# First mixer's scan: the norm of a chunk in three steps behind later chunks' masked scores, and half of the gate's last products on GpSimd

## The chip, the core and the metric

The kernel runs on one core of a Trainium2 chip. The metric is the device time of one execution in microseconds; the time before is the median of three runs.

A core has five engines that each work through their own queue in order: TensorE (PE, its weight loads PEld), VectorE (DVE), ScalarE (ACT), GpSimd (POOL) and SyncE (SP), which here only issues DMA transfers. An instruction that waits holds everything behind it on its engine.

## What is computed

Two layers over 512 latent and 256 context tokens of width 1024: layer 0 mixes with a bidirectional mLSTM, layer 1 with retention, and a mixture of 16 experts follows each mixer. The change touches the end of the first mixer. Its scan sums a forward and a backward pass over chunks, norms every head's row, and gates:

```python
s = jnp.einsum('bhid,bhjd->bhij', qc, kc) * jnp.exp(dmat - m_row[..., None])
num = jnp.einsum('bhij,bhjv->bhiv', s, vc) + w_inter[..., None] * jnp.einsum('bhid,bhdv->bhiv', qc, C)
h = num / jnp.maximum(jnp.abs(den), jnp.exp(-m_row))[..., None]
...
y = y * lax.rsqrt(jnp.mean(y * y, axis=-1, keepdims=True) + EPS)
y = y.reshape(b_, t_, h_ * d_) * norm_g.astype(f32) * jax.nn.sigmoid(o.astype(f32))
return y.astype(o.dtype) @ w_out
```

## The kernel before

The stage lies at some 240 to 390 us of the span. Tokens are cut into six chunks of 128 (order 2, 3, 4, 5, 0, 1), heads into two halves of four (`blk` 0 and 1). In the text "chunk 0" to "chunk 5" count in that order, and a prime marks the second half: chunk 1' is the second chunk of `blk` 1.

`scan0` is a Python generator, one per half. The projections' loop (`Proj.run`) calls it after every step of eight, so its instructions are emitted among the projection's matmuls, the `acc` products (three of 128x512 per step and tile). The first half's scan runs beside the projection of the second half of V and the first gate half, then `states(1)`, then the second half's scan beside the gate's two halves. A scheduler of the language then sets the order on each engine; the lists below show its result.

For a chunk, the scan does this:

- `load` (SP): `qk`, `V`, the decay exponents `E` (two, one per direction) and the weights `qw`, each with two buffers; `load_states` brings the states `Cz`.
- `prep`: GpSimd masks `E` (`affine_select`, L711), ScalarE takes the exponential (eight L715, four per direction), VectorE makes `qw` (L717).
- `scores`: TensorE makes the scores `S0`, `S1` (L725, one buffer each), VectorE makes the masked scores `A0`, `A1` of both directions (four L731).
- `outputs`, once per direction: TensorE makes `num` (L739, L742; two buffers of `num0` and `num1`), VectorE the divisor (`dn`, `rd`: L748, L750, L751); the first direction's quotient `yo` is written by ScalarE (L755), the second's is added by VectorE (L757).
- `normed`: ScalarE squares `yo` (`ysq`, L762), VectorE sums (`yss`, L764, L765), GpSimd raises to the power -1/2 (`yrs`, L766), VectorE multiplies `yo` by it (L767), all emitted directly behind `outputs`.

`o_done` gates a finished tile of the gate's projection: ScalarE's sigmoid `oe` (L636, which frees the `acc` buffer; there are two), GpSimd's product with the norm's gain `ng` (L637), VectorE's product with `yo` (L638), and the store. Sigmoid and exponential need different tables on ScalarE, so a table load lies between them.

`states(1)` makes the second half's states: GpSimd `kw` (L612), TensorE `cu` (L618), VectorE `C` (L622, L624), ten in a row, then stored; `mixer_end` follows with the output projection, from the transposes `yt` on.

Of the kernel before, what the change touches and what calls it, by code (L numbers as in the profile page):

```python
# [2 lines left out]

# [11 lines left out]
OP = mybir.AluOpType  # L15
# [30 lines left out]
def backbone(ctx, tc, x, c, ctx_in, c_ctx, ada_w, ada_b, norm_mix_g, norm_ffn_g, final_norm_g,  # L46
# [3 lines left out]
    nc = tc.nc  # L50
# [5 lines left out]
    def st(name):  # L56
        return small.tile([128, 8], F32, name=name, tag="st", bufs=24)
# [22 lines left out]
    with tc.tile_pool(name="ps0", bufs=1, space=PS, reuse_waits="tile") as ps0, \  # L80
# [24 lines left out]
        for V, vc in ((V1, vc1), (V2, vc2), (VP[:, 0::2], vcp[:, :, 0]), (VP[:, 1::2], vcp[:, :, 1])):  # L105
            n = V.shape[0]
            p = ps0.tile([128, 64], F32, name="pv", bufs=2)
# [397 lines left out]
    order0 = (2, 3, 4, 5, 0, 1)  # L505

    def mlstm_mixer(R):
# [123 lines left out]
        Y, gated = {}, []  # L631

        def o_done(blk, ng):
            def f(tt, p):
                e = pc.tile([128, 512], F32, name="oe", bufs=2)
                nc.scalar.activation(e, p, AF.Sigmoid)  # L636
                nc.gpsimd.tensor_tensor(e, e, ng, op=OP.mult)  # L637
                nc.vector.tensor_tensor(e, e, Y[blk, tt].rearrange("p h v -> p (h v)"), op=OP.mult)  # L638
                nc.sync.dma_start(y_d[0][tt][:, blk * 512:(blk + 1) * 512], e)
                gated.append(tt)  # L640
            return f
# [13 lines left out]
        sb = ctx_w.enter_context(tc.tile_pool(name="scan0", bufs=2, side="right", reuse_waits="tile"))  # L655
        sp = ctx_w.enter_context(tc.tile_pool(name="scanps0", bufs=1, space=PS, side="right", reuse_waits="tile"))
        bg.add(scan0(0, sb, sp, pc, cols, flo, Y, gated), 2)
        P.run(1536, range(6), v_done(1), nxt=2048)
        bg.drain()
        bg.add(seq(states(1, sp, "num0"), scan0(1, sb, sp, pc, cols, flo, Y, gated)))  # L660
        for blk in range(2):
            ng = pc.tile([128, 512], F32, name="ng", bufs=1)
# [7 lines left out]
    def scan0(blk, sb, sp, pc, cols, flo, Y, gated):  # L670

        hs = slice(blk * 4, blk * 4 + 4)
        L = {}
# [6 lines left out]
        def load(cc):  # L680
            t = L[cc] = {}
            t["qk"] = sb.tile([128, 4, 128], F32, name="qk")
            nc.sync.dma_start(t["qk"], dram_ap(qk_d[blk], cc * 128, [[T, 128], [128 * T, 4], [1, 128]]))
            t["V"] = sb.tile([128, 4, 129], F32, name="V")
            nc.sync.dma_start(t["V"], V_d[blk][cc * 128:(cc + 1) * 128])
            t["E"] = sb.tile([128, 2, 4, 128], F32, name="E")
            for d in range(2):
                nc.sync.dma_start(t["E"][:, d], dram_ap(rows_d, (d * H + blk * 4) * T + cc * 128,
                                                        [[0, 128], [T, 4], [1, 128]]))
            ds = [d for d in range(2) if cc in prev0[d]]  # L690
            t["qw"] = sb.tile([128, 2, 2, 128], F32, name="qw")
            for d in ds:
                for h2 in range(2):
                    nc.sync.dma_start(t["qw"][64 * h2:64 * h2 + 64, d],
                                      dram_ap(rows_d, ((2 + d) * H + blk * 4 + h2) * T + cc * 128,
                                              [[0, 64], [2 * T, 2], [1, 128]]))

        def load_states(cc):
            C = L[cc]["C"] = CZ[order0.index(cc) % 2]
            for q in range(2):  # L700
                r = slice(64 * q, 64 * q + 64)
                for d in range(2):
                    if cc in prev0[d]:
                        nc.sync.dma_start(C[r, d, :, q, :], C_d[blk][cc][r, d].rearrange("p (a b) -> p a b", a=2))

        def prep(cc):
            t = L[cc]
            for d in range(2):
                E = t["E"][:, d]
                sg = 1 if d == 0 else -1  # L710
                nc.gpsimd.affine_select(out=E, in_=E, pattern=[[0, 4], [sg, 128]], compare_op=OP.is_ge, fill=BIG,  # L711
                                        base=0, channel_multiplier=-sg)
                for i in range(4):
                    h = blk * 4 + i
                    nc.scalar.activation(E[:, i, :], E[:, i, :], AF.Exp, bias=cols[:, cc, d, h:h + 1], scale=-1.0)  # L715
                if cc in prev0[d]:
                    nc.vector.scalar_tensor_tensor(t["qw"][:, d], t["qk"][:, 0:2], 0.125, t["qw"][:, d],  # L717
                                                   op0=OP.mult, op1=OP.mult)

        def scores(cc):  # L720
            t = L[cc]
            S = [sp.tile([128, 2, 128], F32, name=f"S{q}") for q in range(2)]
            for i in range(4):
                r = slice(64 * (i % 2), 64 * (i % 2) + 64)
                nc.tensor.matmul(S[i % 2][:, i // 2, :], t["qk"][r, 2 + i // 2, :], t["qk"][r, i // 2, :],  # L725
                                 start=True, stop=True)
            for d in range(2):
                A = t["A", d] = sb.tile([128, 2, 2, 128], F32, name=f"A{d}")
                Ev = t["E"][:, d].rearrange("p (g q) i -> p q g i", q=2)
                for q in range(2):  # L730
                    nc.vector.scalar_tensor_tensor(A[:, q], S[q], 0.125, Ev[:, q], op0=OP.mult, op1=OP.mult)  # L731

        def outputs(cc, d, y):
            t = L[cc]
# [22 lines left out]
                        nc.vector.scalar_tensor_tensor(y[:, i, :], num[j][:, q, 0:128], rd[:, q:q + 1], y[:, i, :],  # L757
                                                       op0=OP.mult, op1=OP.add)

        def normed(cc, y):  # L760
            j = sb.tile([128, 4, 128], F32, name="ysq", bufs=1)
            nc.scalar.activation(j, y, AF.Square)  # L762
            ss, rs = st("yss"), st("yrs")
            nc.vector.tensor_reduce(ss[:, 0:4], j, axis=mybir.AxisListType.X, op=OP.add)  # L764
            nc.vector.tensor_scalar(ss[:, 0:4], ss[:, 0:4], 1.0 / 128, EPS, op0=OP.mult, op1=OP.add)  # L765
            nc.gpsimd.tensor_tensor(rs[:, 0:4], ss[:, 0:4], neghalf[:, 0:4], op=OP.pow)  # L766
            nc.vector.tensor_tensor(y, y, rs[:, 0:4, None].to_broadcast([128, 4, 128]), op=OP.mult)  # L767
        load(order0[0])
        load_states(order0[0])
        yield 1  # L770
# [2 lines left out]
        prep(order0[0])  # L773
        yield 1
        scores(order0[0])
        yield 1
        for n, cc in enumerate(order0):
            if n + 2 < len(order0):
                load(order0[n + 2])
            if n + 1 < len(order0):  # L780
                prep(order0[n + 1])
                yield 3
                scores(order0[n + 1])
                yield 4
            while len(gated) < 6 * blk + n - 5:
                yield 1
            y = pc.tile([128, 4, 128], F32, name="yo", bufs=6)
            outputs(cc, 0, y)
            yield 1
            outputs(cc, 1, y)  # L790
            normed(cc, y)
            Y[blk, cc] = y
            if n + 2 < len(order0):
                load_states(order0[n + 2])
            yield 2

    def gates(P, pp, tt_, wgp, gb, cols, flo, wcb, colp):
        ig = tt_("ig")
# [1167 lines left out]
```

## Time and profile before

| | us |
|---|---|
| median of three runs | 1916.28 (1913.15 to 1919.35) |
| the profiled execution | 1921.03 |
| its span, first to last instruction | 1919.2 |
| TensorE busy over the span | 1814.5 (95%) |
| VectorE, ScalarE, GpSimd busy | 730.0, 429.1, 285.3 |
| TensorE busy from 246 to 390 us | 127.97 of 144.00 |

The page gives the busy shares; the waits say which engine waited for whom; a timeline row gives an instruction's start, its length, its engine and line, and in brackets how long the engine stood idle before it and what ended that. Time that an engine other than the bound one stands idle costs nothing by itself.

### The profile page before, as it was taken

The page shows a single profiled execution, that of the slowest core. Times are in us where ns is not written, and L with a number is a line of the kernel's source. Part 1 is how long each engine was busy: PE and PEld are TensorE (multiplying, and loading weights), DVE is VectorE, ACT ScalarE, POOL GpSimd, SP SyncE. Part 2 cuts the span into 40 slices and gives each one's busy share as a digit, 9 for nine tenths or more (in the row PEclk, how much of TensorE's full clock was granted, in tenths as well). Part 3 has the DMA queues.
Part 4 walks back from the last instruction along what each step waited for, and adds up shares of the span by engine and source line. Part 5 has one row for each costly group of instructions (what it writes and reads, how often), then busy time and mean ns, then how long its engine had stood idle before and what let it go on. Part 6 is the DMA issues. An engine that isn't in the chain of part 4 may idle for free. (4 is left out here: it accounts for less than half of the span.)

```text
span 1919.2 us, 27783 instructions
## 1 busy us (share of the span) xinstructions
PE 1814.5 (95%) x11093; PEld 1029.8 (54%) x11093; DVE 730.0 (38%) x1742; ACT 429.1 (22%) x839; POOL 285.3 (15%) x343
## 2 busy tenths in 40 slices
PE   6999988999899999999999999999979999999997
PEld 2765676788444434444444777788764333333332
DVE  3554557646311111111113678454571322222224
ACT  3623356342200000000003621332421010100001
POOL 1110124201121111111001224334200000000001
PEclk9999999999899999999999999999998999999999
DMA  8568777672899999999996588445738999999996
GB/s 273 209 210 273 261 190 206 197 270 84 303 368 391 383 388 398 377 401 379 407 412 234 194 291 274 130 153 188 285 154 306 421 421 420 421 421 421 421 420 247
DMA packets 168578, 585.42 MB, mean 305 GB/s; under 512 B 16674, under 2 KB 68578, under 8 KB 114690
## 3 DMA queue, kind: packets, MB, share of 16 engines
q1 hardware_dynamic: 160176, 570.72, 78.3%
q0 software_dynamic: 6912, 12.71, 3.1%
q8 instruction: 88, 1.44, 0.3%
q10 hardware_dynamic: 1362, 0.23, 0.1%
q14 instruction: 40, 0.33, 0.0%
HBM read 544.13 MB, written 39.47 MB: 304 GB/s over the span
## 5 line engine op out<-in xcount | busy, mean ns | idle before, releaser
L1327 PE MATMUL y<-wslot,hT 128*32 128x256 f32 (+1 forms) x2016 | 278.7, 488 | 8.6 <-ACT hT L1493 8.4
L1327 PE MATMUL gl<-wslot,xs 128*64 128x512 f32 x1024 | 236.2, 605 | 7.1 <-DMA wslot<-in_moe_w_gate_dram 6.1
L1327 PE MATMUL ul<-wslot,xs 128*64 128x512 f32 x1024 | 229.9, 595 | 1.9 <-DMA wslot<-in_moe_w_up_dram 1.9
L312 PE MATMUL acc<-whi,hT_hi 128*128 128x512 f32 x544 | 223.3, 412 | 4.4 <-ACT hT_hi L382 3.1
L313 PE MATMUL acc<-wlo,hT_hi 128*128 128x512 f32 x544 | 218.0, 401 | 0.0
L314 PE MATMUL acc<-whi,hT_lo 128*128 128x512 f32 x544 | 217.3, 399 | 0.2 <-DVE hT_lo L383 0.2
L1327 PEld LDWEIGHTS y<-wslot,hT 128*32 128x32 f32 (+1 forms) x2016 | 100.0, 123 | 171.4 <-issue 131.8
L1476 DVE TENSOR_TENSOR hid<-hid,ul 128x512 f32<-128x512 f32 x32 | 22.0, 688 | 372.5 <-PE ul L1327 372.5
L1327 PEld LDWEIGHTS gl<-wslot,xs 128*64 128x64 f32 x1024 | 71.8, 138 | 155.5 <-issue 134.3
L1327 PEld LDWEIGHTS ul<-wslot,xs 128*64 128x64 f32 x1024 | 71.7, 137 | 148.3 <-issue 136.5
L312 PEld LDWEIGHTS acc<-whi,hT_hi 128*128 128x128 f32 x544 | 102.8, 189 | 39.2 <-issue 9.9
L314 PEld LDWEIGHTS acc<-whi,hT_lo 128*128 128x128 f32 x544 | 103.0, 189 | 28.5 <-issue 4.9
L313 PEld LDWEIGHTS acc<-wlo,hT_hi 128*128 128x128 f32 x544 | 103.4, 190 | 23.4 <-issue 2.8
L1473 ACT ACTIVATE hid<-gl 128x512 f32<-128x512 f32 x32 | 19.1, 598 | 414.9 <-PE gl L1327 414.9
L319 DVE TENSOR_TENSOR wlo<-wslot,whi 128x512 fp32r<-128x512 f32 x108 | 80.1, 758 | 55.8 <-ACT whi L318 55.3
L318 ACT ACTIVATE whi<-wslot 128x512 fp32r<-128x512 f32 x112 | 69.5, 630 | 107.3 <-PE acc L314 101.2
L1507 DVE SCALAR_TENSOR_TENSOR o<-y,gcol,M 128x512 f32<-128x512 f32 (+1 forms) x32 | 19.8, 617 | 143.8 <-PE y L1327 143.8
L1435 POOL TENSOR_TENSOR wslot<-x,wslot 128x512 f32<-128x512 f32 x4 | 5.0, 1277 | 443.3 <-DVE x L1378 443.3
L313 PE MATMUL po<-wol,yh 128*128 128x512 f32 x160 | 65.1, 407 | 2.0 <-DVE wol L319 1.9
L312 PE MATMUL po<-woh,yh 128*128 128x512 f32 x160 | 64.9, 407 | 1.0 <-ACT yh L952 0.8
L314 PE MATMUL po<-woh,yl 128*128 128x512 f32 x160 | 64.3, 403 | 0.0
L1493 ACT ACTIVATE hT<-hp 128x512 f32<-128x512 f32 (+1 forms) x48 | 24.6, 526 | 173.2 <-PE hp L1488 167.5
(450 smaller groups left out, 2517.4 us busy)
## 6 DMA issues: line engine op xcount, KB each, us to landing
wslot<-in_moe_w_up_dram SPq DMA_DIRECT2D x128, 1024.0 KB
wslot<-in_moe_w_gate_dram SPq DMA_DIRECT2D x128, 1024.0 KB
wslot<-in_moe_w_down_dram SPq DMA_DIRECT2D x124, 1024.0 KB
wslot<-in_ada_w_dram SPq DMA_DIRECT2D x40, 1024.0 KB
wslot<-in_ret_w_in_dram SPq DMA_DIRECT2D x16, 1024.0 KB
wslot<-in_mlstm_w_in_dram SPq DMA_DIRECT2D x12, 1024.0 KB
wslot<-in_ada_w_dram SPq DMA_DIRECT2D x16, 512.0 KB
E<-rows_d SPq DMA_DIRECT2D x24, 256.0 KB
```

The costliest lines, as they stand in the source:

```text
L312: nc.tensor.matmul(o, lh, rh, start=first, stop=False)
L313: nc.tensor.matmul(o, lh, rl, start=False, stop=False)
L314: nc.tensor.matmul(o, ll, rh, start=False, stop=last)
L318: nc.scalar.activation(wh, w, AF.Copy)
L319: eng.tensor_tensor(wl, w, wh.bitcast(F32), op=OP.subtract)
L1327: mm = nc.tensor.matmul(o[cw * q:cw * q + cw, :], stat(k), w(k)[:, qn * n:(qn + 1) * n], start=(k == 0), stop=(k == 7), tile_position=(0, ...
L1435: nc.gpsimd.tensor_tensor(O[:, lo], R.X[t][:, lo], fg[:, lo], op=OP.mult)
L1473: nc.scalar.activation(blocks_of(HID[v]), paired(o), AF.Silu)
L1476: nc.vector.tensor_tensor(h, h, paired(o), op=OP.mult)
L1493: LATE["act"] = nc.scalar.activation(HT[v], HP[v], AF.Copy)
L1507: LATE["dve"] = nc.vector.scalar_tensor_tensor(r, o, TOP[v][2][:, e:e + 1], M5[v], op0=OP.mult, op1=OP.mult)
```

## The change

`normed` becomes a generator of three steps. The first, the squares, is taken where `normed` stood. The second (sum, mean, power) is taken after `prep` of the next chunk is emitted, and its sum is placed on VectorE behind the `qw` product of the chunk after that one (`prep`'s mark). The third, the product, is taken after the next `scores`, and is placed on VectorE behind the last masked score of the chunk two further on. What is left open of a chunk when the next one's outputs are done is taken then. In `o_done` the product with `yo` goes to GpSimd for the first half of the heads and stays on VectorE for the second.

```diff
-                nc.vector.tensor_tensor(e, e, Y[blk, tt].rearrange("p h v -> p (h v)"), op=OP.mult)
+                (nc.vector if blk else nc.gpsimd).tensor_tensor(e, e, Y[blk, tt].rearrange("p h v -> p (h v)"), op=OP.mult)
...
-                    nc.vector.scalar_tensor_tensor(t["qw"][:, d], t["qk"][:, 0:2], 0.125, t["qw"][:, d],
-                                                   op0=OP.mult, op1=OP.mult)
+                    t["prep"] = nc.vector.scalar_tensor_tensor(t["qw"][:, d], t["qk"][:, 0:2], 0.125, t["qw"][:, d],
+                                                               op0=OP.mult, op1=OP.mult)
...
-                    nc.vector.scalar_tensor_tensor(A[:, q], S[q], 0.125, Ev[:, q], op0=OP.mult, op1=OP.mult)
+                    t["last"] = nc.vector.scalar_tensor_tensor(A[:, q], S[q], 0.125, Ev[:, q], op0=OP.mult, op1=OP.mult)
...
-        def normed(cc, y):
+        def normed(y, before, after):
             j = sb.tile([128, 4, 128], F32, name="ysq", bufs=1)
             nc.scalar.activation(j, y, AF.Square)
+            yield
             ss, rs = st("yss"), st("yrs")
-            nc.vector.tensor_reduce(ss[:, 0:4], j, axis=mybir.AxisListType.X, op=OP.add)
+            with behind_of(before):
+                nc.vector.tensor_reduce(ss[:, 0:4], j, axis=mybir.AxisListType.X, op=OP.add)
             nc.vector.tensor_scalar(ss[:, 0:4], ss[:, 0:4], 1.0 / 128, EPS, op0=OP.mult, op1=OP.add)
             nc.gpsimd.tensor_tensor(rs[:, 0:4], ss[:, 0:4], neghalf[:, 0:4], op=OP.pow)
-            nc.vector.tensor_tensor(y, y, rs[:, 0:4, None].to_broadcast([128, 4, 128]), op=OP.mult)
+            yield
+            with behind_of(after):
+                nc.vector.tensor_tensor(y, y, rs[:, 0:4, None].to_broadcast([128, 4, 128]), op=OP.mult)
+            yield
+
+        def behind_of(f):
+            ins = f()
+            return tc.issue_after(ins.ins) if ins is not None else contextlib.nullcontext()
...
+        open_ = iter(())
         for n, cc in enumerate(order0):
             if n + 2 < len(order0):
                 load(order0[n + 2])
             if n + 1 < len(order0):
                 prep(order0[n + 1])
+                next(open_, None)
                 yield 3
                 scores(order0[n + 1])
+                next(open_, None)
                 yield 4
...
             outputs(cc, 1, y)
-            normed(cc, y)
+            for _ in open_:
+                pass
+            nx2 = order0[n + 2] if n + 2 < len(order0) else None
+            open_ = normed(y, lambda c=nx2: L[c].get("prep") if c is not None else None,
+                           lambda c=nx2: L[c].get("last") if c is not None else None)
+            next(open_)
             Y[blk, cc] = y
             if n + 2 < len(order0):
                 load_states(order0[n + 2])
             yield 2
+        for _ in open_:
+            pass
```

Where the lists of instructions differ, three places matter to the prediction.

VectorE, at the masked scores of chunk 2 in the first half (`yo_1938`, `yss` and `yrs` belong to chunk 0, `dn_2094` to chunk 1, `A0`, `A1` and `E_1865` to chunk 2); before:

```order
L764 TENSOR_REDUCE yss_1991<-ysq_1989 128x4
L765 TENSOR_SCALAR yss_1991<-yss_1991 128x4
L748 SCALAR_TENSOR_TENSOR dn_2094<-num0_2086,flo_167 128x2
L767 TENSOR_TENSOR yo_1938<-yo_1938,yrs_1992 128x512
L750 TENSOR_TENSOR dn_2094<-num0_2086,dn_2094 128x2
L751 RECIPROCAL rd_2095<-dn_2094 128x2
L748 SCALAR_TENSOR_TENSOR dn_2101<-num1_2087,flo_167 128x2
L731 SCALAR_TENSOR_TENSOR A0_2056<-S0_2050,E_1865 128x256
L717 SCALAR_TENSOR_TENSOR qw_1868<-qk_1861,qw_1868 128x256
L731 SCALAR_TENSOR_TENSOR A0_2056<-S1_2051,E_1865 128x256
L731 SCALAR_TENSOR_TENSOR A1_2059<-S0_2050,E_1865 128x256
```

The same place on VectorE in the changed kernel (line numbers behind `normed` are larger there, the names are the same):

```order
L732 SCALAR_TENSOR_TENSOR A0_2055<-S0_2049,E_1865 128x256
L718 SCALAR_TENSOR_TENSOR qw_1868<-qk_1861,qw_1868 128x256
L732 SCALAR_TENSOR_TENSOR A0_2055<-S1_2050,E_1865 128x256
L732 SCALAR_TENSOR_TENSOR A1_2058<-S0_2049,E_1865 128x256
L718 SCALAR_TENSOR_TENSOR qw_1868<-qk_1861,qw_1868 128x256
L768 TENSOR_REDUCE yss_2032<-ysq_1989 128x4
L732 SCALAR_TENSOR_TENSOR A1_2058<-S1_2050,E_1865 128x256
L769 TENSOR_SCALAR yss_2032<-yss_2032 128x4
L749 SCALAR_TENSOR_TENSOR dn_2094<-num0_2086,flo_167 128x2
L773 TENSOR_TENSOR yo_1938<-yo_1938,yrs_2033 128x512
L751 TENSOR_TENSOR dn_2094<-num0_2086,dn_2094 128x2
L752 RECIPROCAL rd_2095<-dn_2094 128x2
```

The masked scores and chunk 1's divisor have changed sides: the product stood ahead of the masked scores, and now stands behind them; it stands ahead of chunk 1's divisor in both.

GpSimd, between the two halves (`E_2749` is chunk 0', `E_2771` chunk 1', `E_2827` chunk 2'; `kw` belong to `states(1)`, `yrs_2490` to chunk 4, `oe_2863` to the gate tile of chunk 2); before:

```order
L711 AFFINE_SELECT E_2749<-E_2749 128x512
L766 TENSOR_TENSOR yrs_2490<-yss_2489,neghalf_67 128x4
L711 AFFINE_SELECT E_2771<-E_2771 128x512
L637 TENSOR_TENSOR oe_2863<-oe_2863,ng_2546 128x512
L711 AFFINE_SELECT E_2771<-E_2771 128x512
L612 TENSOR_TENSOR kw_2591<-knat_764,cols_166 128x256
L612 TENSOR_TENSOR kw_2608<-knat_764,cols_166 128x256
L711 AFFINE_SELECT E_2827<-E_2827 128x512 x2
L612 TENSOR_TENSOR kw_2625<-knat_764,cols_166 128x256
```

The same place on GpSimd in the changed kernel (`yrs_2533` is chunk 4's, `yo_2248` the normed chunk 2):

```order
L712 AFFINE_SELECT E_2749<-E_2749 128x512 x2
L679 MEMSET Cz1_2740 64x4x129 x2
L613 TENSOR_TENSOR kw_2591<-knat_764,cols_166 128x256
L712 AFFINE_SELECT E_2771<-E_2771 128x512
L613 TENSOR_TENSOR kw_2608<-knat_764,cols_166 128x256
L712 AFFINE_SELECT E_2771<-E_2771 128x512
L638 TENSOR_TENSOR oe_2863<-oe_2863,ng_2546 128x512
L770 TENSOR_TENSOR yrs_2533<-yss_2532,neghalf_67 128x4
L639 TENSOR_TENSOR oe_2863<-oe_2863,yo_2248 128x512
L613 TENSOR_TENSOR kw_2625<-knat_764,cols_166 128x256
```

The fifth `kw` stood behind chunk 2's exponents, and now stands behind chunk 1's second exponent, both gate products and chunk 4's power.

ScalarE, at the end of the second half's scan (`yo_3346` is chunk 4', `oe_3505` and `oe_3513` are the sigmoids of the second gate half's first two tiles); before:

```order
L762 ACTIVATE ysq_3309<-yo_3264 128x512
L636 ACT_TABLE_LOAD
L636 ACTIVATE oe_3505<-acc_3458 128x512
L755 ACTIVATE yo_3346<-num0_3347,rd_3354 128x128 x2
L755 ACTIVATE yo_3346<-num1_3348,rd_3361 128x128 x2
L636 ACTIVATE oe_3513<-acc_3462 128x512
```

The same place on ScalarE in the changed kernel (`yo_3391` is chunk 5'):

```order
L756 ACTIVATE yo_3346<-num0_3347,rd_3354 128x128 x2
L756 ACTIVATE yo_3346<-num1_3348,rd_3361 128x128 x2
L764 ACTIVATE ysq_3389<-yo_3346 128x512
L756 ACTIVATE yo_3391<-num0_3392,rd_3401 128x128 x2
L756 ACTIVATE yo_3391<-num1_3393,rd_3408 128x128 x2
L637 ACT_TABLE_LOAD
L637 ACTIVATE oe_3505<-acc_3458 128x512
L637 ACTIVATE oe_3513<-acc_3462 128x512
```

The table load and the sigmoids, which free the `acc` buffers, stood ahead of chunk 4's quotient, and now stand behind chunk 5's.

## Rows read from the trace of the kernel before

**Rows 1.** The page, part 1: busy us, share of the span, instructions.

```profile
PE 1814.5 (95%) x11093; PEld 1029.8 (54%) x11093; DVE 730.0 (38%) x1742; ACT 429.1 (22%) x839; POOL 285.3 (15%) x343
```

**Rows 2.** Windows: us, length, busy PE PEld DVE ACT POOL, PEclk, DMA share, GB/s.

```profile
246.00:390.00 144.00, 127.97 (x702) 101.86 (x703) 93.08 (x331) 71.69 (x178) 47.11 (x57) 0.94 0.70 205
...
540.00:580.00 40.00, 39.80 (x334) 16.29 (x332) 5.05 (x13) 2.10 (x5) 6.57 (x5) 1.00 1.02 386
...
1700.00:1740.00 40.00, 38.52 (x174) 14.96 (x171) 9.13 (x14) 4.25 (x7) 0.00 (x0) 1.00 1.01 421
```

**Rows 3.** Windows, the stretches of the stage with a lower granted clock.

```profile
265.80:272.50 6.70, 6.60 (x27) 5.38 (x27) 4.75 (x12) 4.77 (x11) 4.66 (x5) 0.50 0.66 157
...
312.60:316.80 4.20, 4.20 (x25) 2.46 (x22) 4.16 (x12) 1.22 (x3) 2.07 (x3) 0.60 0.49 167
...
354.70:361.20 6.50, 6.48 (x25) 5.71 (x26) 5.20 (x25) 5.26 (x14) 1.55 (x2) 0.50 0.75 222
```

**Rows 4.** Waits of PE from 246 to 390 us: total, times, longest.

```profile
PE S L725 <- DVE A L731: 2.8, 1, 2.8
PE S L725 <- DVE dn L750: 2.5, 1, 2.5
PE num L739 <- DVE A L731: 2.3, 1, 2.3
PE cu L618 <- DVE C L624: 1.9, 1, 1.9
...
PE acc L312 <- ACT oe L636: 1.2, 2, 0.8
```

**Rows 5.** Timeline of DVE: start, length, instruction, [idle before <-what ended it].

```profile
260.89 1.14 DVE L767 TENSOR_TENSOR yo<-yo,yrs 128x512 f32<-128x512 f32 x1 [2.69 <-POOL yrs L766]
...
309.67 1.76 DVE L767 TENSOR_TENSOR yo<-yo,yrs 128x512 f32<-128x512 f32 x1 [1.88 <-POOL yrs L766]
...
328.96 1.75 DVE L638 TENSOR_TENSOR oe<-oe,yo 128x512 f32<-128x512 f32 x1 [2.30 <-POOL oe L637]
```

**Rows 6.** Timeline of POOL at chunk 2 and among the states.

```profile
259.20 0.64 POOL L711 TENSOR_SCALAR_AFFINE_SELECT E<-E 128x512 f32<-128x512 f32 x1 [6.78 <-DMA E<-rows_d]
259.80 1.05 POOL L766 TENSOR_TENSOR yrs<-yss,neghalf 128x4 f32<-128x4 f32 x1
260.85 0.63 POOL L711 TENSOR_SCALAR_AFFINE_SELECT E<-E 128x512 f32<-128x512 f32 x1
...
308.06 0.61 POOL L612 TENSOR_TENSOR kw<-knat,cols 128x256 f32<-128x256 f32 x1
...
309.61 1.28 POOL L637 TENSOR_TENSOR oe<-oe,ng 128x512 f32<-128x512 f32 x1
```

**Rows 7.** Timelines of SP and POOL: chunk 5's E loads issued, and masked when landed.

```profile
281.45 0.93 SPq L688 DMA_DIRECT2D E<-rows_d  x2
...
285.52 0.63 POOL L711 TENSOR_SCALAR_AFFINE_SELECT E<-E 128x512 f32<-128x512 f32 x1 [3.75 <-DMA E<-rows_d]
287.49 0.63 POOL L711 TENSOR_SCALAR_AFFINE_SELECT E<-E 128x512 f32<-128x512 f32 x1 [1.34 <-DMA Cz<-C_d]
```

**Rows 8.** Timeline of ACT at chunk 2.

```profile
261.52 1.28 ACT L715 ACTIVATE E<-E,cols 128x128 f32<-128x128 f32 x4 [0.37 <-POOL E L711]
262.70 0.60 ACT L755 ACTIVATE yo<-num,rd 128x128 f32<-128x128 f32 x2
263.32 1.28 ACT L636 ACT_TABLE_LOAD   x1
264.61 0.60 ACT L636 ACTIVATE oe<-acc 128x512 f32<-128x512 f32 x1
```

**Rows 9.** Tiles E and yo, by line: ns min/median/max, first and last start.

```profile
L731 DVE SCALAR_TENSOR_TENSOR A<-S,E x48: 405/416/425, 245.2 to 359.7; 128x256 f32<-128x256 f32 x48
...
L767 DVE TENSOR_TENSOR yo<-yo,yrs x12: 691/693/1760, 260.9 to 376.8; 128x512 f32<-128x512 f32 x12
```

**Rows 10.** Timeline of PE where the gate's last product ends.

```profile
389.39 0.39 PE L314 MATMUL acc<-whi,hT_lo 128*128 128x512 f32 x1
389.62 1.03 PE L950 MATMUL yt<-ident,yg 128*128 128x128 f32 x8
```

More of the change, by code (lines that the diff above doesn't have):

```diff
@@ L1 @@
+import contextlib
 import math
```

## The prediction

> **What bounds the kernel now.** I read the page first: TensorE is busy 1814.5 us, 95% of the span [rows 1], so an edit pays only where TensorE stands idle or runs at its lower clock. Then the windows. In the stage that the change touches, 246 to 390 us, TensorE is busy 127.97 of 144.00 us: 16.0 us idle. Its mean granted clock there is 0.94 [rows 2], 0.06 x 144 = 8.6 us of full-speed work; the rows for the slow stretches agree: 0.50 over 6.7 us, 0.60 over 4.2 and 0.50 over 6.5, so 3.35 + 1.7 + 3.25 = 8.3 us [rows 3], that is the 1.2 GHz level, each time behind idle stretches of TensorE. Idle time and clock together, some 24.6 us or 1.3%, are the ceiling of any edit to this stage.
>
> The waits name what the idle time is. Four single waits for VectorE make up 2.8 + 2.5 + 2.3 + 1.9 = 9.5 us; the sigmoids that free the `acc` buffers add 1.2 [rows 4]. VectorE's timeline tells why it was late at two of the four: the norm's product L767 waited 2.69 us for GpSimd's power at 260.89, with chunk 2's masked scores behind it, and 1.88 us at 309.67, with the state updates behind it [rows 5].
>
> What is saved in the stage reaches the end: the gate's last product at 389.39 is followed by `mixer_end`'s transposes without a wait [rows 10], the first experts keep TensorE busy 39.80 of 40 us, and the last ones are bound by transfers (DMA share 1.01 [rows 2]) whose slots TensorE frees, so they move with it.
>
> **The change part by part.** No instruction of the norm is added or removed: twelve chunks keep their square, sum, scaling, power and product. They change places, and six gate products go from VectorE to GpSimd. I walk the stage with the order lists and the rows' durations; a plus makes the kernel slower.
>
> (a) Chunk 2. The product no longer stands ahead of the masked scores. What is late next is the `acc` buffer: TensorE's list now has ten `acc` products ahead of chunk 3's scores, and the seventh needs a buffer that the sigmoid frees. The sigmoid stands behind chunk 2's exponentials. Before, their last group began at 261.52 and took 1.28; GpSimd's power (1.05) no longer stands between the two masks of `E` [rows 6], so they end between 261.75 and 262.8. With table load 1.28 and sigmoid 0.60 [rows 8] the buffer is free at 263.6 to 264.7. TensorE, idle from 261.03, waits 2.6 to 3.7 us; before it waited 2.3 + 0.8 [rows 4]: -0.5 to +0.6. Chunk 1's divisor now stands behind power and product, and `num` of chunk 2 waits for it: 0 to 1.0 (one power, 1.05). Ends -0.5 and +1.6; I take 0, since the first 0.6 are as likely to come as to go and later products catch up the rest. The slow clock behind it stays.
>
> (b) Chunks 4 and 5. Here the loads of `E` set the pace: issued at 281.45, masked at 285.52 and 287.49, so 4 and 6 us later [rows 7]. Before, a product's wait lay inside that time, ahead of the masked scores. Now it lies behind them and ahead of the next divisor, so the divisor comes later by power 1.05 + product 0.69 - what the scores gain (0.7), about 1.0 for each chunk and 2.5 at the far end for both. Against it, chunk 5's first `E` load no longer queues behind its `V` load, up to 1.0. Ends -1.0 and +2.5; taken +1.0, as one of two chunks.
>
> (c) Chunk 1' 's scores, which waited 2.5 us for chunk 0' 's masks and a divisor [rows 4], now stand among the state products: -2.5. What is late next is the sigmoid that frees `acc` for the next two tiles, behind chunk 5's quotients and a table load: 1.28 + 0.60 [rows 8] less the 0.7 of three `acc` products, 1.2. Ends -2.5 and 0; taken -1.3.
>
> (d) The states. The fifth `kw` now stands on GpSimd behind chunk 1' 's second `E`, the gain product, the power and the gate product. That `E` is issued after chunk 5's `num` ends (its `V` load waits for the buffer) and lands 6 us later; mask 0.63, gain product 1.28, power 1.05, gate product 1.28 (as the gain's), `kw` 0.61 [rows 6] end it at 10.8 us. TensorE asks after 14 `acc` products at 0.23 us, four state groups at 0.52 and the sigmoid's wait, 6.5 us: a stall of up to 4.3 us. The 1.9 us wait of `cu` for `C` [rows 4] stays, since chunk 5's product still stands among the updates. Ends 0 (the load lands at once) and +4.3; I take +2.0, next to the one wait of this kind that the trace has, 1.9.
>
> (e) The six gate products leave VectorE. At 328.96 one held it for 2.30 of waiting and 1.75 of work [rows 5], and TensorE stood 1.2 us behind it. Ends -1.2 and 0; taken -1.2.
>
> (f) Chunk 4'. TensorE waited 2.8 us for its masked scores [rows 4], and 6.5 us at half clock follow [rows 3]. Now these scores don't wait for the product, and chunk 4' 's first `E` load goes ahead of its `V`; what is late next is the landing, which leaves about 1.1 of the 2.8. Ends -2.8 - 3.25 = -6.0 and 0; taken -1.7 for the wait and half the clock's 3.25, -1.7: -3.4.
>
> (g) The second gate half's first sigmoids now stand behind chunk 5' 's quotients, with the table load between: about 3.3 us after `num`, of which TensorE covers 1.8 with the rest of `num` and four `acc` products. Ends 0 and +1.5; taken +1.5, as the list leaves no other cover.
>
> Sum: 0 + 1.0 - 1.3 + 2.0 - 1.2 - 3.4 + 1.5 = -1.4 us. The ends sum to -11.2 and +9.9. The profiled execution, 1919.2 us of span and 1.8 around it, is 1921.03; with -1.4 it would be 1919.6. It lay 4.75 us above the median, so on the median's scale the forecast is 1916.28 - 1.4 = 1914.9 us: no change that can be told. A measurement of this kernel tells about 0.3% apart, 5.7 us: faster is below 1910.5, slower above 1922.0.
>
> **The rivals.** First, the freed masked scores pay and nothing takes their place: all terms at their low ends, -11.2, gives 1905.1. For it: the four waits are single and VectorE's queue is their cause; TensorE's list has more `acc` products ahead of `num` in most chunks. Against it: a chunk's `E` load takes 4 to 6 us whatever VectorE does [rows 7], and the list leaves more `acc` products for after the scan, so fewer cover it.
>
> Second, GpSimd's queue becomes the bound: term (d) at its end, 4.3 instead of 2.0, the idle time drops TensorE to its lower clock for a stretch like the last one, 3.25 [rows 3], and the scan then runs too late for the gain of (f), 3.4. That is -1.4 + 2.3 + 3.25 + 3.4 = +7.6, so 1923.8 us. It decides once the fifth `kw` starts over 4 us after TensorE asks. For it: every step ahead of `kw` has its row. Against it: TensorE's list has scores and `acc` products beside the states that could shift.
>
> Third, GpSimd's products hold VectorE. A product of the norm takes 0.69 at the median and 1.76 at most [rows 9], and the longest, at 309.67, ran beside a GpSimd product at 309.61 [rows 5, 6]: 1.07 more. Six products more on GpSimd would cost 6 x 1.07 = 6.4 us of VectorE, and 1921.3 us if all of it reached TensorE. The masked scores aren't held: 48 of them took 405 to 425 ns [rows 9], so little of it would. The Trainium skill, "SBUF — State Buffer", section "Who interferes with whom", says that a VectorE instruction with two inputs in SBUF and a GpSimd instruction that reads SBUF exclude each other for a whole instruction. The two rows agree with it, and it speaks against the second part of the change; by that rule each of the six can cost its full length, 1.28, or 7.7 us.
>
> **How the numbers follow.** Forecast 0.38, first rival 0.36, second 0.20, third 0.06 (it ends within 0.3%). So faster 0.36, within 0.3% 0.38 + 0.06 = 0.44, slower 0.20. The likeliest case's own range, ends halved as they don't fall together, is 1910 to 1920. The range for 8 in 10 reaches over most of both rivals: 1903 to 1924.
>
> **What would show it.** In the changed kernel's trace: VectorE's masked scores of chunks 2 and 4' without a wait for the power in front (right for a, f); `acc` behind the sigmoid near 264 and near chunk 5' (a, g); the fifth `kw` behind `E` of chunk 1' with TensorE's `cu` idle before it (d); TensorE busy from 246 to the last `acc` product near 127 us with about 15 us idle. If that idle time falls under 10 us, or no stretch of the stage has the lower clock, the forecast is wrong towards faster; if `cu` alone waits over 4 us, towards slower.

## The result and the profile after

The changed kernel is slower: 1931.93 us at the median of six runs (1926.21 to 1935.42) against 1919.85 for the kernel before beside it, a ratio of 1.0061 (95% interval 1.0042 to 1.0081). A second series gave 1.0054 (1.0033 to 1.0076). On the scale of the forecast that is 1916.28 x 1.0061 = 1928.0 us, where 1914.9 was forecast and 1903 to 1924 was the range. The traced execution was the changed kernel's fastest, 1926.21 us, while that of before was one of its slower, 1921.03. So the two traces show only 5 of the 12 us between the medians; the changed kernel's six executions alone spread over 9 us, and the ratios below decide.

The page, part 1, of the changed kernel:

```profile
PE 1807.9 (94%) x11093; PEld 1025.3 (53%) x11093; DVE 730.5 (38%) x1736; ACT 428.6 (22%) x839; POOL 293.1 (15%) x349
```

Its windows: the stage, and the stretches with a lower clock (columns as in [rows 2]):

```profile
246.00:390.00 144.00, 119.25 (x662) 94.23 (x663) 91.58 (x324) 70.31 (x176) 55.55 (x62) 0.92 0.64 186
...
264.50:271.50 7.00, 6.09 (x24) 4.71 (x25) 5.85 (x19) 4.36 (x11) 6.25 (x6) 0.55 0.61 157
306.80:317.40 10.60, 9.89 (x53) 6.49 (x53) 5.37 (x17) 0.88 (x2) 3.93 (x6) 0.54 0.58 186
343.80:350.20 6.40, 3.62 (x13) 3.24 (x14) 5.70 (x23) 4.20 (x13) 2.04 (x3) 0.50 0.66 196
```

TensorE is busy 119.25 of the 144 us, 8.7 less than in [rows 2]: the stage ends later. The three slow stretches cost 0.45 x 7.0 + 0.46 x 10.6 + 0.5 x 6.4 = 11.2 us of clock, against 8.3 in [rows 3].

The places where TensorE waited for more than 1 us from 262 us on, from the timeline of the changed kernel:

```profile
264.51 0.50 PE L313 MATMUL acc<-whi,hT_hi 128*128 128x512 f32 x1 [3.45 <-ACT oe L637]
...
286.50 0.71 PE L743 MATMUL num<-V,A 128*128 128x129 f32 x4 [1.47 <-ACT yo L756]
...
294.21 0.70 PE L740 MATMUL num<-Cz,qw 128*128 128x258 f32 x2 [1.14 <-DMA E<-rows_d]
...
301.21 0.66 PE L619 MATMUL cu<-V,kw 128*64 128x129 f32 x8 [1.29 <-DVE dn L751]
...
307.51 1.13 PE L619 MATMUL cu<-V,kw 128*64 128x129 f32 x8 [3.25 <-DVE C L623]
...
329.82 0.67 PE L740 MATMUL num<-Cz,qw 128*128 128x258 f32 x2 [1.56 <-DMA Cz<-C_d]
...
346.58 1.23 PE L740 MATMUL num<-Cz,qw 128*128 128x258 f32 x2 [5.55 <-ACT yo L756]
...
360.16 0.68 PE L726 MATMUL S<-qk 64*128 64x128 f32 x4 [1.37 <-DVE dn L749]
...
376.02 0.50 PE L313 MATMUL acc<-whi,hT_hi 128*128 128x512 f32 x1 [1.68 <-ACT oe L637]
```

Two of them have a slow stretch behind them that the kernel before didn't have, or had at less than half the length (4.2 us against 10.6). **Among the states** (307.51) the timelines of GpSimd and VectorE read so:

```profile
302.53 0.63 POOL L712 TENSOR_SCALAR_AFFINE_SELECT E<-E 128x512 f32<-128x512 f32 x1
303.13 1.28 POOL L638 TENSOR_TENSOR oe<-oe,ng 128x512 f32<-128x512 f32 x1
304.37 1.01 POOL L770 TENSOR_TENSOR yrs<-yss,neghalf 128x4 f32<-128x4 f32 x1
305.35 1.27 POOL L639 TENSOR_TENSOR oe<-oe,yo 128x512 f32<-128x512 f32 x1
306.57 1.06 POOL L613 TENSOR_TENSOR kw<-knat,cols 128x256 f32<-128x256 f32 x1
...
305.41 1.75 DVE L773 TENSOR_TENSOR yo<-yo,yrs 128x512 f32<-128x512 f32 x1 [2.42 <-POOL yrs L770]
307.09 0.28 DVE L623 COPY C<-cu 128x129 f32<-128x129 f32 x1
```

Chunk 4's power starts at 304.37, behind a mask and a gain product; VectorE's norm product waits 2.42 us for it and runs 1.75 us, beside the gate product that started on GpSimd at 305.35; the copy that frees TensorE's `cu` buffer stands behind it. The fifth `kw` starts at 306.57, behind the gate product; by its row it ends at 307.63, the copy at 307.37, so the two are late side by side.

**In the second half's scan** (346.58), the timelines of GpSimd, VectorE and ScalarE:

```profile
337.02 1.43 POOL L638 TENSOR_TENSOR oe<-oe,ng 128x512 f32<-128x512 f32 x1 [4.87 <-ACT oe L637]
338.54 1.62 POOL L639 TENSOR_TENSOR oe<-oe,yo 128x512 f32<-128x512 f32 x1
340.12 1.79 POOL L638 TENSOR_TENSOR oe<-oe,ng 128x512 f32<-128x512 f32 x1
341.98 1.26 POOL L639 TENSOR_TENSOR oe<-oe,yo 128x512 f32<-128x512 f32 x1
343.20 1.01 POOL L770 TENSOR_TENSOR yrs<-yss,neghalf 128x4 f32<-128x4 f32 x1
344.17 1.67 POOL L712 TENSOR_SCALAR_AFFINE_SELECT E<-E 128x512 f32<-128x512 f32 x2
...
344.24 1.11 DVE L773 TENSOR_TENSOR yo<-yo,yrs 128x512 f32<-128x512 f32 x1 [3.46 <-POOL yrs L770]
345.27 0.15 DVE L749 SCALAR_TENSOR_TENSOR dn<-num,flo 128x2 f32<-128x2 f32 x1
...
344.84 0.40 ACT L716 ACTIVATE E<-E,cols 128x128 f32<-128x128 f32 x1 [5.07 <-POOL E L712]
345.91 1.14 ACT L756 ACTIVATE yo<-num,rd 128x128 f32<-128x128 f32 x4 [0.67 <-DVE dn L749]
```

Four products of the last two gate tiles hold GpSimd from 337.0 to 343.2. Behind them stand the power of chunk 0', for which VectorE waits with chunk 1' 's divisors behind, and the masks of chunk 3', for which ScalarE waits with chunk 1' 's quotients behind. Chunk 2' 's `num` needs the buffer that these quotients read.

The same place on TensorE in the kernel before: two short waits in chunk 1' 's `num`, and none ahead of chunk 2' 's at 339.26.

```profile
332.00 0.67 PE L739 MATMUL num<-Cz,qw 128*128 128x258 f32 x2 [0.71 <-PE num L742]
...
334.02 0.67 PE L739 MATMUL num<-Cz,qw 128*128 128x258 f32 x2 [0.48 <-DVE yo L757]
...
339.26 0.70 PE L739 MATMUL num<-Cz,qw 128*128 128x258 f32 x2
```

### The profile page after: what moved, and what is told of

Read it like the earlier page. It is cut to its first block, busy times and chain, and to the rows that moved or that the text cites. A ratio compares the mean times of both kernels' runs of the same rounds, so it can differ in the third digit from the quotient of the medians.

```text
span 1924.4 us, 27804 instructions
## 1 busy us (share of the span) xinstructions
PE 1807.9 (94%) x11093; PEld 1025.3 (53%) x11093; DVE 730.5 (38%) x1736; ACT 428.6 (22%) x839; POOL 293.1 (15%) x349
```

## The experiments

All ratios are to the kernel before, run beside on the same chip.

**Which part.** Each part alone, and the steps without their placement. The three edits, of the changed kernel (e1, e3; e4 is both), and of the kernel before (e2):

```diff
e1
-                (nc.vector if blk else nc.gpsimd).tensor_tensor(e, e, Y[blk, tt]...
+                nc.vector.tensor_tensor(e, e, Y[blk, tt]...
e2
-                nc.vector.tensor_tensor(e, e, Y[blk, tt]...
+                (nc.vector if blk else nc.gpsimd).tensor_tensor(e, e, Y[blk, tt]...
e3
-            return tc.issue_after(ins.ins) if ins is not None else contextlib.nullcontext()
+            return contextlib.nullcontext()
```

> The norm in three steps as in the changed kernel, the gate's last product on VectorE in both halves as before. Theory G (the GpSimd queue: gate products stand there ahead of the norm's power and of the state weights kw, and the norm's product on VectorE, with the divisors behind it, waits for that power): the 5.6 us wait of num and the half clock behind it (about 2 us) go, the 3.3 us wait of cu shrinks to the 1.9 us of the kernel before; ratio to the kernel before 0.998 to 1.002. Theory N (the placement of the norm's product behind the masked scores and ahead of the divisor costs by itself): most of the loss stays, ratio 1.004 to 1.006.

> The kernel before with only the gate's last product on GpSimd in the first half. Theory G in its strict form (the loss needs both parts: a long GpSimd queue and a product that waits for a power in it ahead of divisors): ratio 1.000 to 1.002, as the power then has no gate product ahead of it and only the exponents' masks and kw move by 1.3 us each. Theory N: 0.999 to 1.000, as the products leave VectorE. A third theory C (GpSimd's products lengthen VectorE's two-input work beside them): 1.002 to 1.004, and longer VectorE instructions beside the products.

> The changed kernel with the three steps emitted as they are, but without the two placements on VectorE behind the marks of later chunks. Theory G: power and gate products still meet on GpSimd, so the loss stays, 1.004 to 1.007. Theory N: the product stands ahead of the masked scores again or where the scheduler finds it free, and the loss goes, 0.999 to 1.002.

> The norm in three steps without the placements and with the gate's last product on VectorE in both halves. Theory G: no gate product more on GpSimd, ratio 0.998 to 1.002. Theory N: as without the placements, 0.999 to 1.001. Both agree here; the kernel tells what the placements are worth beside e1: by theory N it is 0.4% faster than e1, by theory G within 0.2%.

Measured:

| | ratio | 95% interval |
|---|---|---|
| e2: gate's product alone | 1.0003 | 0.9988 to 1.0018 |
| e1: norm in steps alone | 1.0014 | 0.9998 to 1.0030 |
| the same again | 1.0022 | 1.0008 to 1.0035 |
| both: the changed kernel | 1.0061, 1.0054 | 1.0042 to 1.0081, 1.0033 to 1.0076 |
| e3: both, no placement | 1.0034 | 1.0019 to 1.0048 |
| e4: steps, no placement | 0.9997 | 0.9984 to 1.0009 |

The parts' effects don't add: 0.0003 + 0.0018 = 0.0021 against 0.0057, so some 0.35%, 7 us, comes from having both. The move of the products takes some 0.4% with the placement or without it (the changed kernel against e1, e3 against e4), and nothing that can be told where the norm isn't in steps (e2). The placement takes about 0.2% with either gate. GpSimd's products as such cost nothing that can be told (e2), which speaks against theory C. The mean of e1 is at the upper end of theory G and far from theory N's 1.004; e3, at 1.0034, lies between the two theories' figures.

Why the same four products do no harm in e2: there the sigmoids of these tiles stand ahead of chunk 2' 's exponentials on ScalarE, the block runs from 326.7 to 332.1, and the power of chunk 0' comes after it with time to spare. The timeline of GpSimd in e2:

```profile
326.72 2.50 POOL L637 TENSOR_TENSOR oe<-oe,ng 128x512 f32<-128x512 f32 x2 [11.39 <-ACT oe L636]
329.18 2.94 POOL L638 TENSOR_TENSOR oe<-oe,yo 128x512 f32<-128x512 f32 x2
332.08 1.21 POOL L711 TENSOR_SCALAR_AFFINE_SELECT E<-E 128x512 f32<-128x512 f32 x2
334.93 1.01 POOL L766 TENSOR_TENSOR yrs<-yss,neghalf 128x4 f32<-128x4 f32 x1 [1.64 <-DVE yss L765]
```

**Which tiles, and whether one power is the link.** Of the changed kernel; e7 gives `normed` a flag that is false for chunk 0':

```diff
e5
-                (nc.vector if blk else nc.gpsimd).tensor_tensor(e, e, Y[blk, tt]...
+                (nc.vector if blk or tt < 2 else nc.gpsimd).tensor_tensor(e, e, Y[blk, tt]...
e6
+                (nc.gpsimd if not blk and tt < 2 else nc.vector).tensor_tensor(e, e, Y[blk, tt]...
e7
-            nc.gpsimd.tensor_tensor(rs[:, 0:4], ss[:, 0:4], neghalf[:, 0:4], op=OP.pow)
+            if power:
+                nc.gpsimd.tensor_tensor(rs[:, 0:4], ss[:, 0:4], neghalf[:, 0:4], op=OP.pow)
+            else:
+                rs = ss
```

> The changed kernel, but the gate's last product of the last two gate tiles of the first half (tokens 0 and 1) is on VectorE, the other four stay on GpSimd. Theory G2 (the loss is made in the second half's scan, at 337 to 350 us: two gain and two gate products stand ahead of the power of chunk 0', VectorE's norm product waits for it with the divisors of chunk 1' behind, num of chunk 2' waits 5.6 us and runs at half clock): num's wait falls to about 1.5 to 2.6 us as in the kernels without gate products on GpSimd, ratio 1.001 to 1.003. Theory G1 (the loss is made among the states at 306 to 317 us, where the fifth kw stands behind a gate product and the half clock lasts long): the wait of cu and the half clock there stay, ratio 1.004 to 1.006.

> The mirror of the one before: only the last two tiles' gate products on GpSimd, the first four on VectorE. Theory G2: the 5.6 us wait of num stays, 1.003 to 1.005. Theory G1: the kw queue is short again and the loss goes, 1.000 to 1.002. If the two effects add, the differences of this and the one before from the kernel with neither (1.0014) sum to the changed kernel's 0.0047.

> The changed kernel with one instruction less: the power of chunk 0' (second half, first chunk) is left out, and the norm's product of that chunk multiplies by the mean square itself, so that this chunk's rows are not normed. All gate products stay on GpSimd. Theory G2: VectorE's product no longer waits for GpSimd at 344 us, the wait of num falls from 5.6 to at most 2.5 us and its half clock (2 us) goes; 4 to 6 us are won, ratio 1.003 to 1.004. Theory G1, or a loss by GpSimd's reads beside VectorE: one instruction of 1.0 us on GpSimd is nothing, 1.005 to 1.006.

Measured: e5 1.0034 (1.0018 to 1.0050), e6 1.0015 (1.0001 to 1.0030), e7 1.0060 (1.0039 to 1.0082). Theory G2 falls in the form stated: the last two tiles alone cost nothing beside e1, and without the power nothing comes back. But theory G1 doesn't hold as stated either: e5 lies between the two theories' figures, and e5 and e6 exceed e1's mean by 0.0016 and -0.0003, which doesn't add up to the changed kernel's loss. The trace of e7 shows why: VectorE is free of the wait, and ScalarE now ends last, by the mask behind the same four products. Timelines of ScalarE, GpSimd and TensorE in e7:

```profile
345.68 0.40 ACT L716 ACTIVATE E<-E,cols 128x128 f32<-128x128 f32 x1 [4.27 <-POOL E L712]
345.99 1.12 ACT L756 ACTIVATE yo<-num,rd 128x128 f32<-128x128 f32 x4
...
343.80 1.26 POOL L639 TENSOR_TENSOR oe<-oe,yo 128x512 f32<-128x512 f32 x1
345.01 1.22 POOL L712 TENSOR_SCALAR_AFFINE_SELECT E<-E 128x512 f32<-128x512 f32 x2
...
346.65 1.05 PE L740 MATMUL num<-Cz,qw 128*128 128x258 f32 x2 [4.25 <-ACT yo L756]
```

**Taking products out.** Left out, not moved, of the changed kernel:

```diff
e9 (e10 puts the gain product under the condition too; e11 has "tt != 4")
+                if blk or tt >= 2:
-                (nc.vector if blk else nc.gpsimd).tensor_tensor(e, e, Y[blk, tt]...
+                    (nc.vector if blk else nc.gpsimd).tensor_tensor(e, e, Y[blk, tt]...
```

> The changed kernel without the gate's last product of the last two gate tiles of the first half (left out, not moved: these tiles are stored with sigmoid times gain alone). Theory G3 (one GpSimd block of two gain and two gate products, 337.0 to 343.2 us, is waited for by two engines at once: VectorE by the power of chunk 0' and ScalarE by the mask of chunk 3', and both hold chunk 1' 's quotients, so taking away the power alone gains nothing): the block is 2.9 us shorter, num's wait falls from 5.6 to about 2.7 us, ratio 1.0035 to 1.005. Rival S (what costs is where the scheduler puts the sigmoids of these tiles on ScalarE, late behind chunk 2' 's exponentials; the products behind them don't matter): 1.0055 to 1.0065.

> The same with the gain products of these two tiles left out too, so that the whole block is gone from GpSimd (the tiles are stored as bare sigmoids). Theory G3: the wait of num is 1 us at most, the half clock behind it goes, ratio 1.002 to 1.0035, what is left being the norm's steps (1.0014) and the states. Rival S: 1.0055 to 1.0065. Theory G1 (the states' kw queue makes the loss): 1.005 to 1.006.

> The changed kernel without the gate's last product of the third gate tile alone (token chunk 4, the one that stands ahead of the fifth kw; left out, not moved). Theory G1: kw starts 1.3 us earlier, cu's wait of 3.3 us falls to 2.0, the half clock from 307 to 317 us (5.3 us lost) shrinks by a half, ratio 1.002 to 1.004. Theory G3: only the 1.3 us are won, ratio 1.005 to 1.006.

> The changed kernel once more, beside the three ablations on the same chip: ratio 1.0045 to 1.0075 by every theory; it is what the three are read against.

Measured: e9 1.0045 (1.0029 to 1.0060), e10 1.0059 (1.0039 to 1.0079), e11 1.0056 (1.0038 to 1.0073), e12 1.0054 (1.0033 to 1.0076). None is told from the changed kernel. Theory G3's figure for e10 was wrong, and theory G1's for e11: without the gate product ahead of the fifth `kw` TensorE still waited 2.88 us for `cu`. Rival S's figure holds for e10 and not for e9; no run moves the late sigmoids by themselves, so that rival stays open for this place. With the block gone GpSimd waits for chunk 3' 's exponents, and the power stands behind that mask. Timelines of GpSimd and TensorE in e10:

```profile
342.20 0.63 POOL L713 TENSOR_SCALAR_AFFINE_SELECT E<-E 128x512 f32<-128x512 f32 x1 [7.85 <-DMA E<-rows_d]
342.80 1.01 POOL L771 TENSOR_TENSOR yrs<-yss,neghalf 128x4 f32<-128x4 f32 x1
...
345.77 0.70 PE L741 MATMUL num<-Cz,qw 128*128 128x258 f32 x2 [3.03 <-ACT yo L757]
```

So a transfer was the third thing that was late there, and the wait fell by 2.5 us only.

**The states.** Of the changed kernel (g3: of e10), with a flag of `normed` that is false for chunk 4 of the first half; g2 leaves out its power as e7 did for chunk 0', g1 and g3 its product; g4 is e1 again:

```diff
g1, g3
+            if not full:
+                return
             with behind_of(after):
                 nc.vector.tensor_tensor(y, y, rs[:, 0:4, None].to_broadcast([128, 4, 128]), op=OP.mult)
```

> The changed kernel without VectorE's norm product of chunk 4 in the first half (that chunk's rows are not normed), which waits 2.4 us for the power at 305 us and runs 1.75 us with the state copies C behind it. Theory K (the clock: the wait of cu among the states is what drops TensorE to half speed for 10 us, 5 us lost, and that is the larger part of the loss): cu waits 1 us at most, the clock loss among the states falls from 5.25 to 1.75 us or less, 3 us of idle and 3.5 of clock are won, ratio 1.002 to 1.003. Rival M (many small terms, none above 2 us): 1.0045 to 1.0055.

> The changed kernel without GpSimd's power of chunk 4 in the first half (the product multiplies by the mean square; that chunk's rows are not normed). The product stays on VectorE and no longer waits behind the gain product and the power. Theory K: cu's wait falls from 3.3 us to about 1.2 (the product's own 0.7 to 1.75 us stays), ratio 1.002 to 1.004. Rival M: 1.005 to 1.006.

> The changed kernel without the norm product of chunk 4 and without the four gate products of the last two tiles of the first half (as e10). If the states (theory K) and the block at 337 to 343 us together are the loss: 0.999 to 1.001. Rival M: 1.003 to 1.005.

> The norm's steps with the gate's last product on VectorE, once more, beside the others. Theory K: ratio 1.000 to 1.003 again, idle time of TensorE up to the output projection near 22 us and clock loss under 8 us. If the first profile was a lucky execution, its clock loss is 10 to 16 us as in the changed kernel, and the ratio 1.003 to 1.005.

Measured: g1 1.0026 (1.0014 to 1.0037), g2 1.0030 (1.0015 to 1.0046), g3 1.0014 (1.0003 to 1.0026), g4 1.0022 (1.0008 to 1.0035). Here one instruction of 1.0 us on GpSimd (g2) is worth some 0.3%, about half of the loss, and with the block of the second half out as well (g3) the kernel stands where the norm alone stands. So by these ratios the states are the larger place, and the block is worth some 0.12% (g1 to g3), which is within these two intervals. The same power and product were not taken out of e1 or of the kernel before, so what leaving them out gains there, without the gate's products on GpSimd, is not known.

The wait itself didn't go in g1, against theory K. Its releaser changed to the fifth `kw`, which stands behind mask, gain product, power and gate product. In g2 the wait was 1.82 us. Timelines of TensorE and GpSimd in g1:

```profile
310.91 1.04 PE L619 MATMUL cu<-V,kw 128*64 128x129 f32 x8 [4.06 <-POOL kw L613]
...
306.82 1.27 POOL L638 TENSOR_TENSOR oe<-oe,ng 128x512 f32<-128x512 f32 x1
308.04 1.01 POOL L770 TENSOR_TENSOR yrs<-yss,neghalf 128x4 f32<-128x4 f32 x1
309.02 1.27 POOL L639 TENSOR_TENSOR oe<-oe,yo 128x512 f32<-128x512 f32 x1
310.24 1.19 POOL L613 TENSOR_TENSOR kw<-knat,cols 128x256 f32<-128x256 f32 x2
```

What differs is the clock around it. The window from the first to the last `cu`, of the changed kernel:

```profile
298.36:321.07 22.71, 18.01 (x106) 11.55 (x106) 14.11 (x40) 10.49 (x20) 13.68 (x16) 0.77 0.53 160
```

Of the changed kernel in its second series:

```profile
296.19:318.06 21.87, 16.99 (x107) 10.90 (x106) 13.39 (x40) 10.26 (x20) 13.67 (x16) 0.84 0.58 165
```

Of g1:

```profile
300.91:319.64 18.73, 12.44 (x97) 7.84 (x97) 11.54 (x38) 11.92 (x24) 12.53 (x17) 0.91 0.68 173
```

And of e1:

```profile
300.70:320.07 19.37, 13.66 (x107) 9.06 (x107) 14.13 (x39) 11.54 (x21) 11.41 (x15) 1.00 0.59 177
```

Length times (1 - granted clock) is what the clock takes: 5.2 and 3.5 us in the changed kernel, 1.7 in g1, none in e1. The table does the same for the stage from the first scores (some 240 us) to the output projection's first transposes, and its last column for the states alone; idle is length less TensorE's busy time. Idle time inside a slow stretch is counted as idle and as clock, so the columns don't add up to the length.

| one trace of | its execution | ratio | length | idle | taken by the clock | of that, states |
|---|---|---|---|---|---|---|
| before | 1921.03 | 1 | 149.6 | 16.0 | 9.0 | 1.7 |
| changed | 1926.21 | 1.0061 | 158.5 | 25.1 | 12.7 | 5.2 |
| changed again | 1924.38 | 1.0054 | 155.4 | 22.7 | 10.9 | 3.5 |
| e1, norm alone | 1922.48 | 1.0014 | 151.8 | 22.9 | 4.6 | 0 |
| the same again | 1922.32 | 1.0022 | 150.0 | 19.0 | 7.5 | 1.8 |
| e2, gate alone | 1914.67 | 1.0003 | 147.2 | 15.0 | 7.4 | 0.1 |
| e3, no placement | 1920.44 | 1.0034 | 150.5 | 17.5 | 9.0 | 3.4 |
| e4, steps without placement | 1915.20 | 0.9997 | 146.2 | 16.0 | 5.8 | 3.5 |
| e5, first four products | 1922.81 | 1.0034 | 152.6 | 21.2 | 6.1 | 0 |
| e10, block out | 1929.01 | 1.0059 | 158.0 | 22.9 | 12.6 | 5.1 |
| g1, product of chunk 4 out | 1926.07 | 1.0026 | 157.4 | 24.5 | 12.6 | 1.7 |
| g2, power of chunk 4 out | 1932.64 | 1.0030 | 160.0 | 23.3 | 16.0 | 3.5 |
| g3, both places out | 1918.28 | 1.0014 | 148.2 | 20.5 | 4.4 | 0 |

In these traces the norm's steps with their placement bring 3 to 7 us of idle time. With the gate's product on GpSimd there are 0 to 6 us more of it, and the clock takes 11 to 13 us instead of 5 to 8. But single traces can lie far off: g2's execution was the slowest of its eight, and g1's took as long as the changed kernel's and lost as much to the clock, at other places of the stage, though the ratios tell the two kernels apart. The states' column doesn't follow the ratios either: e4 loses nothing and has 3.5 us there, e5 is at 1.0034 and has none. So that the clock among the states makes the loss is not shown; that about half of the loss goes with chunk 4's norm is.

**A version that might beat both**, e4 with the gain's product in the first half on VectorE too:

```diff
-                nc.gpsimd.tensor_tensor(e, e, ng, op=OP.mult)
+                (nc.gpsimd if blk else nc.vector).tensor_tensor(e, e, ng, op=OP.mult)
```

> A version that might beat both: the three steps without placements, and in the first half both gate products, the gain's too, on VectorE, so that GpSimd has only masks, powers and kw there. By theory G every product taken from GpSimd's queue shortens the waits of kw and power: e4 measured 0.9997 with 2.6 us at cu and 2.6 us at num left; both shrink by up to 1.3 us and the ratio is 0.997 to 0.999. By the rival that VectorE becomes the bound (six products of 0.69 us more, 4.1 us): 1.000 to 1.002.

Measured: 0.9994 (0.9980 to 1.0009), no difference that can be told, from before or from e4; theory G's 0.997 to 0.999 did not come.

## Why the prediction was wrong, step by step

The places of the sum can be read in the two traces; a plus makes the kernel slower.

| term | forecast (ends) | measured | rows |
|---|---|---|---|
| (a) chunk 2 | 0 (-0.5 to +1.6) | +1.3 | 3.45 + 0.90 us against 3.1 |
| (b) chunks 4, 5 | +1.0 (-1.0 to +2.5) | +1.6 | three waits, 3.2 against 1.6 |
| (c) chunk 1' 's scores | -1.3 (-2.5 to 0) | -1.0 | 1.5 at `cu` against 2.5 |
| (d) states, idle | +2.0 (0 to +4.3) | +1.4 | 3.25 against 1.9 |
| (d) states, clock | none | +3.2 | 0.46 x 10.6 against 1.7 |
| (e) gate products | -1.2 (-1.2 to 0) | -1.2 | waits of 0.71 and 0.48 gone |
| no term: four products on GpSimd | none | +5.6 and +3.2 | 5.55, none before; clock 0.5 x 6.4 |
| (f) chunk 4' | -3.4 (-6.0 to 0) | -4.6 | 1.4 against 2.75; no slow stretch |
| (g) second gate half's sigmoids | +1.5 (0 to +1.5) | +1.7 | 1.68 at 376.02 |

**Right:** (b), (c), (f) and (g) went the way and near the size forecast, and (a) went as its mechanism said: TensorE waited 3.45 us where 2.6 to 3.7 had been worked out. Its mistake was to let the extra go.

**The step that failed is (e)**, "the six gate products leave VectorE", whose ends were -1.2 and 0. The gain that it names came: the 1.2 us behind the product at 328.96 are the waits at 332.00 and 334.02 (the sigmoids' two waits of [rows 4], 1.2 us too, had ended ahead of it, at 265.26 and 326.29), and they are gone. But it costed the engine that the products leave, and nothing on the engine that they join. With the norm in steps their move costs some 7 us: 1.0061 and 1.0054 against 1.0014 and 1.0022 of e1. One place is seen in the trace, the wait of 5.55 us. The block of four was in the order lists, with chunk 0' 's power and chunk 3' 's masks behind it; the walk looked at GpSimd among the states alone, in (d). The term's upper end should have held the block's growth, two products of 1.28, and the idle time with a slow stretch behind it. What this place is worth alone is not shown: e9 and e10 gave back nothing that can be told.

**Mis-sized is (d):** its wait is about as forecast, but a slow stretch of 10.6 us follows, 4.9 us of clock against 1.7 before, and no term had it. g1 and g2 show that about half of the loss goes with chunk 4's norm in this place; that it is the clock which carries it is not shown. The 1.9 us wait for `C` and the fifth `kw` weren't one behind the other, as the step added them, but side by side: the wait ends with `C` in the changed kernel, with `kw` in g1.

**The second rival comes nearest:** power, gate products and `kw` were late in GpSimd's queue, the clock fell behind the wait of `cu`, and it stood at 1923.8 us. But its condition did not hold: the fifth `kw` started 2.3 us after TensorE asked (at 304.26), not over 4. It was priced too low since the second place wasn't in it, and it held (f)'s gain for lost, which came. The third rival did not decide: e2 has all six products on GpSimd and 1.0003. The row that it was built on came again: the norm product at 305.41 took 1.75 us beside the GpSimd product that began 0.06 us ahead of it, where 0.69 is the median [rows 9]. That agrees with the Trainium skill, "SBUF — State Buffer", section "Who interferes with whom". It is at most 1.06 us of the wait there, and e11, without that GpSimd product, gave nothing back that can be told.

**Not settled:** why TensorE's clock falls for 10.6 us behind the wait of `cu` in the changed kernel and not in e1's first trace, where that wait is 2.90 us and others stand around it. The traces of the changed kernel, e7, e9, e10 and e11, all at 1.0045 or above, lose 3.5 to 5.2 us to the clock among the states, but e3, e4 and g2 lose 3.4 to 3.5 there too; which property of the idle time decides, and what it is worth, wasn't tried. Nor is it shown why the two edits together cost more than each alone: that they meet in GpSimd's queue is read from the traces, and half of the loss is tied to a place. The part of the loss that the norm with its placement makes alone, 0.14 to 0.22%, was not taken apart further; e4 shows that it hangs on the placement.

## What to carry to other kernels

When work is moved from one engine to another, cost it on the engine that it joins, at each place where it lands, by what stands behind it there and who waits for that; an engine that is busy 15% of the time can still have a full queue for 6 us. Two edits that each cost little can cost more together: by the traces one made a product wait for GpSimd with other engines' work behind it, and the other made GpSimd late. Where two or three chains end within a microsecond or two of each other, taking one away gives back little, as e7 and e10 show, so price a place by its second-latest chain.

## What the hardware showed that had not been expected

In the two traces of each, the changed kernel and the norm alone differ more in what the granted clock takes (12.7 and 10.9 us against 4.6 and 7.5) than in idle time (25.1 and 22.7 us against 22.9 and 19.0). A wait of much the same length came with a slow stretch in one kernel and without one in another: 10.6 us of it at the 3.25 us wait of `cu` in the changed kernel, none at the 2.90 us in e1. So a trace's idle time alone doesn't give what its waits cost, and g1's row shows that the clock of one trace doesn't give it either.
